# A two-layer decoder trunk on one core: the instruction order made with the scheduler's other machine model

## The chip, the cores and the metric

The kernel runs on one core of one Trainium2 chip. The metric is the device time of one execution in microseconds (us), as the median of several runs. Engines are named as in the profile: PE (TensorE, the matrix engine; its weight loads are PEld), DVE (VectorE), ACT (ScalarE), POOL (GpSimd), SP (SyncE, which here only issues transfers; SPq is its queue).

## The reference, cut to what matters

Two layers of a decoder over 256 tokens of width 1024, all in float32. Each layer runs three token mixers on the same input and adds them through gates, then a feed-forward network:

```
p = x @ w_in[l]                                   # one wide projection for all mixers
y_a = rwkv7_time_mix(...)                         # recurrence over tokens, 8 heads of 64
y_b = mla_branch(...)                             # latent attention, 8 heads, blocks of 128 queries
y_c = s5_branch(...)                              # diagonal state space, 32 groups x 64 states
merged = g0 * y_a + g1 * y_b + g2 * y_c           # sigmoid gates, also from p
x = layer_norm(ALPHA * x + merged @ w_out[l])
h = silu(x @ ffn_w1[l]) * (x @ ffn_w3[l])         # width 2816
x = layer_norm(ALPHA * x + h @ ffn_w2[l])
```

## The kernel before, in words

**The weight stream.** Almost all of the matrix work is one stream of weight chunks of 128 x 1024 floats (512 KB), 138 a layer, in the order in which the program uses them. `w_load` (lines 156 to 173) handles one chunk: SyncE issues its load into `raw` (line 160, three buffers), ScalarE casts it to a rounded high part `whi` (line 161), and VectorE subtracts to get the low part `wlo` (line 171; for some chunks GpSimd takes the last eighths, line 173). `whi` and `wlo` have four buffers each. A projection (`mm3`, lines 206 to 208) makes three matmuls for each 128 x 128 block: high times high, high times the input's low part, low times high. One chunk in this form is 8 blocks, 24 matmuls of 256 columns.

**The stages of a layer.** First the inputs of the mixers are projected (`rw_unit`, `s5_in`, `latents`), with the state space scan (`s5_tile`, lines 717 to 774) between. Then comes the mixing stage, a list of steps in `ORDER2`: preparation of the recurrence (`prep`), its scores, the inverse of its triangular blocks (`inverse`), its `solve` (lines 1018 to 1077), its normalization (`norm`, line 1103 near its end), attention, and projections and gates of the stream (`glu_unit`, `branch1`, `gate_pair`, `branch0`). `branch0`, four chunks a layer, needs the recurrence's result; the other projections don't. Then `token_major` multiplies by `w_out` (lines 510 to 512) and applies the layer norm, the feed-forward network's first part runs in 22 pieces, and `token_major` again multiplies by `ffn_w2`.

**A solve** goes over four blocks of 64 tokens, one after the other. In each, TensorE makes a right-hand side (lines 1031 and 1035), ScalarE copies it from PSUM into `Gc`, TensorE multiplies it by the inverse (line 1043), VectorE copies the result into `ST`, and for three of the four blocks TensorE makes the next state (lines 1053 and 1055), which VectorE scales in two halves (line 1059). There are two solves in each layer.

**The tables of the state space model.** `s5_tables` builds them; for layer 1 GpSimd does it during layer 0's feed-forward stage (lines 384 to 389 are the rotation that doubles the cosine and sine tables). For layer 0 the work is shared, with VectorE and ScalarE taking part (lines 404 to 418).

**What sets the order.** The program is written in one order, and every instruction gets its rank from its place there. When the `TileContext` closes, a scheduler puts the instructions of each engine into their final order. It plays the program through on a model of the machine: whenever the model says that an engine can take an instruction, the scheduler gives it, among those whose inputs and buffers the model says are there, the one that comes first in the program. The order so found is fixed in the program; on the chip each engine takes its instructions strictly in that order and waits at the head for what is not there yet. SyncE's transfers are ordered in the same way, so a load that waits for its buffer holds up the loads behind it. In `token_major`, lines 516 to 518 load the two rows of the layer norm and the tokens; their buffers in the feed-forward stage of layer 0 lie where the tables' temporary tiles lay.

A few instructions tie the order by hand: `gate` (in `w_load` and `layer_norm`) makes some chunk subtractions wait for a layer norm's statistics, and `issue_after` keeps four ScalarE instructions behind another.

## Time and profile before

| | |
|---|---|
| time, median of 3 runs | 1072.03 us (1067.92 to 1077.68) |
| the profiled execution's own time | 1068.97 us |
| its span, first to last instruction | 1067.1 us |
| granted TensorE clock, mean | 0.986 of full |
| PE, PEld, DVE, ACT, POOL busy | 1014.2, 912.5, 784.7, 482.6, 235.2 us |
| read from memory | 156.72 MB, 151 GB/s over the span |

The times are device times; the span is what the trace covers, 1.9 us less than that execution's time. Busy time is time in which at least one instruction of the engine is in flight. Matmuls overlap in a pipeline, so a busy TensorE is not one at its peak.

### The profile page before, as it was taken

The numbers are of one execution on the slowest core, as the hardware profiler recorded it, in microseconds if no ns is written. First come the engines' busy times: TensorE is split into PE (matmuls) and PEld (weight loads), VectorE is DVE, ScalarE is ACT, GpSimd is POOL, SyncE is SP. The second block draws the span as 40 slices with busy tenths as digits, with TensorE's granted clock in tenths as the row PEclk, the third lists the DMA queues.
The fourth block names the chain that finished last, engine by engine and source line by source line (L and its number), as shares of the span: only waits on it lengthen the run. The fifth ranks groups of instructions, "written<-read, shape, count | busy, mean of one in ns | idle before, by whom it ended". The sixth has DMA issues, their size and how long they took to land.

```text
span 1067.1 us, 21219 instructions
## 1 busy us (share of the span) xinstructions
PE 1014.2 (95%) x8560; PEld 912.5 (86%) x8560; DVE 784.7 (74%) x1542; ACT 482.6 (45%) x797; POOL 235.2 (22%) x262
## 2 busy tenths in 40 slices
PE   8799989999999999799999999999999999999997
PEld 7798778888896999798878999778889879999885
DVE  7969978976578778386474998888747876667546
ACT  5544477534244244144325346865334423443431
POOL 2970222300000599500012003221002420000000
PEclk9989999999999999999999999999999999999999
DMA  8442241223385555466536325232234755555562
GB/s 280 156 159 90 91 147 41 92 89 100 93 294 177 197 180 171 162 207 217 185 123 218 126 81 191 79 98 85 76 100 173 252 190 215 183 188 183 179 196 79
DMA packets 47394, 163.86 MB, mean 154 GB/s; under 512 B 5696, under 2 KB 8256, under 8 KB 46400
## 3 DMA queue, kind: packets, MB, share of 16 engines
q1 hardware_dynamic: 47008, 161.98, 45.9%
q8 instruction: 67, 1.10, 0.4%
q10 hardware_dynamic: 288, 0.52, 0.1%
q14 instruction: 31, 0.25, 0.1%
HBM read 156.72 MB, written 4.19 MB: 151 GB/s over the span
## 4 chain that ended last, share of the span: by engine, by line
PE 58%; DVE 17%; POOL 9%; DMA 7%; ACT 5%; issue 3%; SPq 0%; DVEq 0%; ACTq 0%; POOLq 0%
PE mm L208 11%; PE mm L207 10%; PE mm L206 10%; DMA raw<-in_ws 6%; DVE wlo L171 3%; PE mm L511 3%; PE mm L512 3%; PE mm L510 3%; ACT whi L161 3%; DVE z L745 1%; PE pa L726 1%; PE pb L1035 1%; POOL st L387 1%; PE pb L1043 1%; PE pa L940 1%
## 5 line engine op out<-in xcount | busy, mean ns | idle before, releaser
L171 DVE TENSOR_TENSOR wlo<-raw,whi 128x1024 fp32r<-128x1024 f32 (+2 forms) x265 | 333.5, 1262 | 171.8 <-ACT whi L161 169.1
L161 ACT CAST whi<-raw 128x1024 fp32r<-128x1024 f32 (+2 forms) x267 | 277.4, 1043 | 379.8 <-PE mm L207 211.8
L206 PE MATMUL mm<-xh,whi 128*128 128x256 f32 x1312 | 376.9, 287 | 14.2 <-ACT whi L161 13.9
L208 PE MATMUL mm<-xh,wlo 128*128 128x256 f32 x1312 | 376.1, 287 | 2.9 <-DVE wlo L171 2.6
L207 PE MATMUL mm<-xl,whi 128*128 128x256 f32 x1312 | 375.1, 286 | 0.4 <-DVE xl L262 0.4
L206 PEld LDWEIGHTS mm<-xh,whi 128*128 128x128 f32 x1312 | 249.2, 190 | 18.6 <-ACT whi L161 14.5
L208 PEld LDWEIGHTS mm<-xh,wlo 128*128 128x128 f32 x1312 | 250.2, 191 | 7.6 <-DVE wlo L171 4.0
L207 PEld LDWEIGHTS mm<-xl,whi 128*128 128x128 f32 x1312 | 250.2, 191 | 2.7 <-DVE xl L262 0.6
L240 POOL TENSOR_TENSOR rs<-rs,mhalf 128x1 f32<-128x1 f32 x8 | 7.8, 971 | 341.2 <-DVE rs L238 341.2
L206 PE MATMUL mm<-yh,whi 128*128 128x256 f32 x256 | 74.6, 291 | 0.1
L207 PE MATMUL mm<-yl,whi 128*128 128x256 f32 x256 | 74.1, 289 | 0.0
L208 PE MATMUL mm<-yh,wlo 128*128 128x256 f32 x256 | 74.1, 289 | 0.0
L511 PE MATMUL mm<-wlo,hh 128*128 128x512 f32 x132 | 52.0, 394 | 0.0
L510 PE MATMUL mm<-whi,hh 128*128 128x512 f32 x132 | 51.7, 394 | 0.0
L512 PE MATMUL mm<-whi,hl 128*128 128x512 f32 x132 | 51.5, 392 | 0.0
L206 PEld LDWEIGHTS mm<-yh,whi 128*128 128x128 f32 x256 | 48.5, 189 | 2.3 <-ACT qa L113 0.9
L207 PEld LDWEIGHTS mm<-yl,whi 128*128 128x128 f32 x256 | 48.5, 190 | 1.2 <-issue 0.8
L208 PEld LDWEIGHTS mm<-yh,wlo 128*128 128x128 f32 x256 | 48.6, 190 | 1.1 <-issue 0.7
L240 POOL TENSOR_TENSOR rsn<-rsn,mhalf 128x8 f32<-128x8 f32 x4 | 6.5, 1634 | 142.8 <-DVE rsn L238 142.8
L173 POOL TENSOR_TENSOR wlo<-raw,whi 128x384 fp32r<-128x384 f32 (+2 forms) x24 | 27.7, 1162 | 44.6 <-ACT whi L161 42.5
L947 POOL TENSOR_SCALAR_AFFINE_SELECT Mk<-Mk 64x512 f32<-64x512 f32 x32 | 27.0, 844 | 43.6 <-ACT Mk L113 42.3
L510 PEld LDWEIGHTS mm<-whi,hh 128*128 128x128 f32 x132 | 24.8, 188 | 6.2 <-DVE th L1284 0.8
(487 smaller groups left out, 1745.7 us busy)
## 6 DMA issues: line engine op xcount, KB each, us to landing
raw<-in_ws SPq DMA_DIRECT2D x267, 512.0 KB, 3.8
raw<-in_ws SPq DMA_DIRECT2D x8, 416.0 KB, 3.5
xd<-xk SPq DMA_DIRECT2D x3, 1024.0 KB, 4.1
xk<-xd SPq DMA_DIRECT2D x3, 1024.0 KB, 7.4
lg<-in_lnv SPq DMA_DIRECT2D x4, 512.0 KB, 5.0
lb<-in_lnv SPq DMA_DIRECT2D x4, 512.0 KB, 5.7
pc<-in_spC SPq DMA_DIRECT2D x2, 768.0 KB, 5.3
pb<-in_spB SPq DMA_DIRECT2D x2, 512.0 KB, 4.9
```

What stands on the lines that cost most here:

```text
L161: S.copy(out=hi[:, s], in_=raw[:, s])
L171: V.tensor_tensor(out=lo[:, 0:m], in0=raw[:, 0:m], in1=hi[:, 0:m].bitcast(F32), op=ALU.subtract)
L173: G.tensor_tensor(out=lo[:, m:w], in0=raw[:, m:w], in1=hi[:, m:w].bitcast(F32), op=ALU.subtract)
L206: PE.matmul(ps, lhsT=wh, rhs=xh, start=first, stop=False)
L207: PE.matmul(ps, lhsT=wh, rhs=xl, start=False, stop=False)
L208: PE.matmul(ps, lhsT=wl, rhs=xh, start=False, stop=last)
L240: G.tensor_tensor(out=out, in0=in_, in1=mh(out), op=ALU.pow)
L387: E.tensor_tensor(out=s1, in0=c0, in1=ls, op=ALU.mult)
L510: PE.matmul(acc[b][n], lhsT=ah, rhs=w[0][:, s], start=(k == 0), stop=False)
L511: PE.matmul(acc[b][n], lhsT=ah, rhs=w[1][:, s], start=False, stop=False)
L512: PE.matmul(acc[b][n], lhsT=al, rhs=w[0][:, s], start=False, stop=(k == nk - 1))
L947: G.affine_select(out=Mk[r, h], in_=Mk[r, h], pattern=[[0, 4], [1, 2], [1, 64]], compare_op=ALU.is_ge, fill=0.0, base=-1, channel_multipli ...
```

## The change: one argument of the context

The scheduler has two models of the machine. By default it plays the program on the first, a simulator that runs each instruction for a modelled duration. The argument chooses the second, a timeline simulator with its own durations for instructions, transfers and queues. The program that is traced is the same, instruction by instruction; buffers are given out and waits are set along the new order. Nothing else differs.

```
@@ -1499,7 +1499,7 @@
         arrays[f"in_{name}"] = a
         args.append(nc.dram_tensor(f"in_{name}", a.shape, mybir.dt.from_np(a.dtype), kind="ExternalInput").ap())
     out = nc.dram_tensor("out_0", (T, D), F32, kind="ExternalOutput").ap()
-    with tile.TileContext(nc) as tc:
+    with tile.TileContext(nc, schedule_with_timeline_sim=True) as tc:
         trunk(tc, *args, out)
     r = _run(nc, [arrays], core_ids=[0])
     return r.results[0]["out_0"].reshape(1, T, D)
```

## Rows read from the trace of the kernel before

**Rows 1.** The page's first part: busy us (share of the span) and instructions, each engine.

```profile
span 1067.1 us, 21219 instructions
...
PE 1014.2 (95%) x8560; PEld 912.5 (86%) x8560; DVE 784.7 (74%) x1542; ACT 482.6 (45%) x797; POOL 235.2 (22%) x262
```

**Rows 2.** Windows of 27 us: length, busy time and instructions, clock, DMA.

```profile
108.00:135.00 27.00, 23.21 (x277) 20.28 (x276) 27.00 (x52) 13.19 (x22) 7.30 (x6) 1.00 0.30 96
270.00:297.00 27.00, 25.57 (x243) 23.30 (x242) 14.59 (x24) 8.66 (x13) 1.64 (x1) 1.00 0.40 135
918.00:945.00 27.00, 27.00 (x228) 27.00 (x227) 18.18 (x29) 11.62 (x15) 0.00 (x0) 1.00 0.57 179
```

**Rows 3.** Waits of PE: waiter, awaited, us in total, times, longest.

```profile
PE mm L206 <- ACT whi L161: 13.9, 3, 6.8
PE pc L1094 <- DVE yT L1089: 3.1, 2, 1.7
```

**Rows 4.** Around 442 us: SPq's wait, timelines (start, length) of SP, ACT, PE.

```profile
SPq L516 <- POOL st L389: 15.5, 1, 15.5
...
442.81 0.33 SPq L516 DMA_DIRECT2D lg<-in_lnv  x1
...
452.44 1.04 ACT L161 CAST whi<-raw 128x1024 fp32r<-128x1024 f32 x1 [16.28 <-DMA raw<-in_ws]
...
453.54 0.58 PE L206 MATMUL mm<-xh,whi 128*128 128x256 f32 x1 [6.83 <-ACT whi L161]
```

**Rows 5.** Around 50 us: timelines of ACT and PE.

```profile
48.67 1.33 ACT L418 ACTIVATE cd<-pb,c 128x512 f32<-128x512 f32 x2 [4.98 <-DVE pb L408]
...
51.35 0.58 PE L206 MATMUL mm<-xh,whi 128*128 128x256 f32 x1 [5.62 <-ACT whi L161]
```

**Rows 6.** Windows around the two long waits; the clock follows POOL's busy time.

```profile
42.00:81.00 39.00, 30.94 (x276) 29.41 (x276) 26.35 (x31) 18.54 (x30) 30.63 (x22) 0.82 0.43 147
439.00:467.00 28.00, 20.70 (x157) 20.20 (x156) 11.51 (x19) 7.99 (x10) 3.62 (x3) 0.88 0.63 225
```

**Rows 7.** One solve's block, 271 to 275 us: timeline of all engines.

```profile
271.76 0.44 PE L1035 MATMUL pb<-ST,Mk 64*64 64x64 f32 x4
...
272.30 0.37 ACT L113 COPY Gc<-pb 64x256 f32<-64x256 f32 x1 [5.91 <-PE pb L1035]
...
272.60 0.28 PE L207 MATMUL mm<-xl,whi 128*128 128x256 f32 x1
...
272.80 0.68 PE L1043 MATMUL pb<-Gc,DTf 64*64 64x64 f32 x8
...
273.51 0.43 DVE L113 COPY ST<-pb 64x256 f32<-64x256 f32 x1 [3.18 <-PE pb L1043]
...
274.13 0.28 PE L208 MATMUL mm<-xh,wlo 128*128 128x256 f32 x1
...
274.34 0.27 PE L1055 MATMUL pb<-ST,BKt 128*64 128x64 f32 x1
```

**Rows 8.** Groups by line: count, busy us, mean ns, idle before, its cause.

```profile
L113 DVE COPY ST<-pb 64x256 f32<-64x256 f32 x16 | 6.7, 421 | 24.1 <-PE pb L1043 24.1
...
L1059 DVE TENSOR_TENSOR S<-pb,gam 64x128 f32<-64x128 f32 x24 | 6.9, 289 | 6.5 <-PE pb L1055 6.3
...
L113 ACT COPY Gc<-pb 64x256 f32<-64x256 f32 x16 | 5.9, 366 | 35.2 <-PE pb L1035 35.1
```

**Rows 9.** The weight stream in the feed-forward stage: timeline of PE.

```profile
479.82 0.28 PE L206 MATMUL mm<-xh,whi 128*128 128x256 f32 x1
479.94 0.28 PE L207 MATMUL mm<-xl,whi 128*128 128x256 f32 x1
```

**Rows 10.** The recurrence's last step and the next stage's first (min/median/max ns, first to last start).

```profile
289.65 1.06 PE L1103 MATMUL pc<-dg,pc 128*128 128x256 f32 x4
...
L510 PE MATMUL mm<-whi,msh x24: 388/396/501, 319.3 to 341.2; 128*128 128x512 f32 x24
...
813.24 1.02 PE L1103 MATMUL pc<-dg,pc 128*128 128x256 f32 x4
...
L510 PE MATMUL mm<-whi,msh x24: 387/389/796, 842.7 to 865.6; 128*128 128x512 f32 x24
```

**Rows 11.** Line 171 at 351 to 437 us and at 891 to 1000 us.

```profile
L171 DVE TENSOR_TENSOR wlo<-raw,whi x28: 1210/1378/2287, 350.4 to 433.3; 128x1024 fp32r<-128x1024 f32 x28
...
L171 DVE TENSOR_TENSOR wlo<-raw,whi x38: 1224/1228/1230, 890.6 to 997.1; 128x1024 fp32r<-128x1024 f32 x38
```

More of the change, by code (lines that the diff above doesn't have):

```diff
@@ L1501 @@
     out = nc.dram_tensor("out_0", (T, D), F32, kind="ExternalOutput").ap()
-    with tile.TileContext(nc) as tc:
+    with tile.TileContext(nc, schedule_with_timeline_sim=True) as tc:
         trunk(tc, *args, out)
```

## The prediction

> **What bounds the kernel now.** I read the views from the whole to the single wait. The page's first part: TensorE (PE) has work in flight for 1014.2 of 1067.1 us, 95%, and no other engine comes near [rows 1]. So a new order can hardly win by emptying another engine; it wins or loses in what TensorE does between its first and last matmul. The table of windows then says where those 53 us lie. In the feed-forward stage (918 to 945 us) TensorE is busy 27.00 of 27.00 us at full clock: nothing there is waiting for an order. In the mixing stage (108 to 135, 270 to 297) it is busy 23.21 and 25.57, and in the first of these VectorE (DVE) is full, 27.00 of 27 [rows 2]. The list of waits names one large group: three waits of TensorE for ScalarE's cast of a weight chunk, 13.9 us together, the longest 6.8 [rows 3]. Everything else is under 3.2 us.
>
> Two of these waits are faults of order, and a scheduler's faults are what this change can touch. At 453.54 us TensorE stands 6.83 us. The SyncE queue shows why: its load of the layer-norm row (line 516) waits 15.5 us for GpSimd's table work (line 389), because the row's buffer takes that work's space, and weight loads stand behind it in the same queue; they go out from 444.18 on, and the cast that TensorE needs starts only at 452.44 [rows 4]. The old model believed GpSimd done earlier than it was. At 51.35 us TensorE stands 5.62 us: ScalarE had stood 4.98 us at line 418 for a VectorE result, and the cast was queued behind it [rows 5]. After both, the granted clock is low: 0.82 over 42 to 81 us and 0.88 over 439 to 467, a mean of time at 2.4 and at 1.2 GHz [rows 6].
>
> **What the change does, part by part.** It removes no instruction and adds none: every duration in the trace stays, up to contention. It moves all of them that are free to move, on five engines and on the SyncE queue, which carries all weight loads. What moves is the choice, each time an engine is free, among instructions that the model believes ready. The trace shows one execution of one order, so each term is a price for an order that fits less or better.
>
> *The recurrence's steps.* Here the present order fits closely, and this is the term that decides. Look at the solve at 271 to 275 us: TensorE's step of line 1035 begins its last group at 271.76 and runs 0.44; ScalarE copies its result (0.37); line 1043 starts at 272.80. Between them lie stream matmuls of lines 206 to 208 that fill just this gap, the last starting at 272.60. The same holds across VectorE's copy of 0.43 at 273.51: stream matmuls to 274.13, then line 1055 at 274.34 [rows 7]. The old model puts each step within some 0.2 us of where the chip can take it. There are 16 such copies by ScalarE, 16 by VectorE, and 24 state updates in 12 pairs [rows 8]: 16 + 16 + 12 = 44 round trips from TensorE to another engine and back, 22 a layer.
>
> An order from other durations can miss in two ways. Too early: the step stands at the head while the copy runs, and TensorE idles for the gap that is now filled, 272.20 to 272.80 = 0.6 us; 44 x 0.6 = 26 us, paid in full since TensorE is the bound. Too late: the step stands behind stream matmuls that were ready first. A weight chunk is 24 matmuls (8 blocks, three products) starting 0.12 us apart [rows 9], 2.88 us, so half a chunk is 1.44 us; 22 x 1.44 = 31.7 us a layer on the chain. TensorE does stream work meanwhile, so this costs only what the stream can't cover at the end. That cover is to be seen: the last step of the recurrence (line 1103) is at 289.65 and 813.24, its matmuls through at about 290.7 and 814.3; the next stage (line 510) starts at 319.3 and 842.7 [rows 10]. Of these 28.5 us, 4 chunks (the `branch0` units) need the recurrence's result, 4 x 2.88 = 11.5; the rest, 17 us, can be done earlier. So 31.7 - 17 = 14.6 us a layer, 29 in both. The bounds: 0 if every step is met as well as now, 2 x (22 x 2.88 - 17) = 93 us if each stands behind a whole chunk. I take 29, close to the 26 of the other way of missing. A gain in this stage is not excluded: the page's PE row leaves 53 us in all, and 41 us of it are not the two faults.
>
> *The two faults.* At best both go: 6.83 + 5.62 = 12.5 us, and the half clock after them. The clock is worth at most (1 - 0.82) x 39 = 7 us and (1 - 0.88) x 28 = 3.4 us [rows 6], together 23 us. At worst both stay, 0, or the misplaced load lands elsewhere on a chunk that is needed at once. I take the first gone and the second kept: -6.8.
>
> A page bears on whether the first goes. In this trace VectorE's subtraction of a weight chunk takes a median 1378 ns, up to 2287, while GpSimd builds the tables, and 1228 (1224 to 1230) where GpSimd is idle [rows 11]; so the two engines stretch each other here. The Trainium skill, "SBUF — State Buffer", section "Who interferes with whom", says that a VectorE instruction with two SBUF inputs and a GpSimd instruction that reads SBUF exclude each other, the later one blocking fully. By that rule a model that prices each engine alone, however well, still sees GpSimd finish too early, the load keeps its place, and the sum would be 6.8 us higher.
>
> *The SyncE queue and VectorE.* Loads that change places cost nothing in the feed-forward stage, where chunks lie ready ahead of TensorE [rows 2]. In the mixing stage VectorE is the cover that is gone: at 27.00 of 27 any chunk subtraction that it takes late is late for TensorE by its own 1.2 us [rows 11]. I put 0 for it in the sum and a rival below.
>
> **The sum.** Against the profiled execution's 1068.97 us: -6.8 + 29.2 = 1091.4. The median of the runs shown, 1072.03, is 3.1 above that execution; so 1094.
>
> **Rivals.** *Faster: the other model is nearer to the chip.* Its place is the SyncE queue at 442 us and ScalarE at 48 us; it decides if lines 516 to 518 are issued behind the weight loads and the cast ahead of line 418, while the 44 steps fit as now. Price: -12.5 us alone gives 1060, with the clock 1049. For it: both faults come from wrong durations. Against it: in the recurrence the old durations were right, so there is little to win besides. Chance 0.30.
>
> *No difference.* The new order is nearly the old one, or a fault removed is paid for by a few steps missed (10 steps too early are 6 us): 1061 to 1083, most likely 1069. For it: the feed-forward stage is full whatever the order [rows 2]. Chance 0.28.
>
> *Slower by another way: starved stream.* A load whose buffer is not yet free is put ahead of weight loads, as at 442 us, at two or three more places, at 7 us each: 1086 to 1093. Its mark would be new waits of TensorE for line 161 or 171 over 5 us, with the recurrence unchanged. Chance 0.08.
>
> **How the numbers follow.** The forecast (steps of the recurrence missed) has 0.34, its own range 1083 to 1128: from half its price to nearly twice. The whole range reaches down over no difference and over most of the faster case, to 1046, and up to 1128; outside stay the best of the faster case and whole-chunk misses, 0.2 together. About 1% is what a measurement here can tell from no change (1061 to 1083). Faster by over 1%: 0.30; within 1%: 0.28; slower: 0.34 + 0.08 = 0.42.
>
> **What would show it.** Right: TensorE's busy time per 27 us falls in 190 to 300 and 710 to 820 us; the waits of ScalarE's `Gc` and VectorE's `ST` copies for lines 1035 and 1043, 35.1 and 24.1 us now [rows 8], grow by some tens of us, or TensorE shows new waits for them; line 510 starts over 10 us later than at 319.3 and 842.7. First fault gone: line 516 issued without a 15 us wait, no 6.8 us gap. Wrong: the recurrence's stretch keeps its length, or shrinks, and the time falls with the two gaps.

## The result, and the profile after

The changed kernel takes 1180.05 us in the median (1177.56 to 1182.24), the kernel before, run beside it, 1073.64; the ratio is 1.0977 (95% interval 1.0931 to 1.1023). No instruction was added to or taken from an engine (the counts below are those of before), so these 106 us are all order. The forecast had the sign right and the size wrong: 1094, with 1128 as its upper end.

The page's first part of the kernel after:

```profile
span 1179.3 us, 21250 instructions
...
PE 1057.5 (90%) x8560; PEld 948.8 (80%) x8560; DVE 792.1 (67%) x1542; ACT 482.4 (41%) x797; POOL 231.8 (20%) x262
```

Against [rows 1] TensorE stands still for 121.8 us where it was 52.9, 69 us more, and the same 8560 matmuls are in flight for 43 us longer; together these are the 112 us of the span. TensorE's share falls only from 95% to 90%, so the share hides a good part of the loss. The Trainium skill, "Perfetto Trace Analysis", section "Identifying the Most-Contended Engine", says that TensorE's matmul busy share is not a good measure of how close a kernel is to roofline, because matmuls are pipelined. For comparing two runs the trace adds a second reason, the clock, below.

Where the loss is, is read from stages. The table is worked out from the first and last starts of TensorE's lines in the two traces: line 851 opens the recurrence's preparation, line 1103 closes its normalization, line 490 is the layer norm's transpose, line 1300 the feed-forward network's first transpose, a few microseconds behind its first matmuls. Differences are taken before rounding.

| stage, us | before | after | difference |
|---|---|---|---|
| start to line 851 | 139.5 | 144.2 | +4.7 |
| mixing, layer 0: to the last of 1103 | 150.8 | 213.4 | **+62.5** |
| to the first of 490 (rest of the stream, `w_out`) | 54.4 | 43.4 | -11.0 |
| layer norm, to 1300 | 11.9 | 16.1 | +4.2 |
| feed-forward, to 490 | 193.1 | 194.4 | +1.3 |
| to line 851 of layer 1 | 114.3 | 115.8 | +1.5 |
| mixing, layer 1 | 149.8 | 199.7 | **+49.8** |
| to 490 | 55.1 | 46.6 | -8.5 |
| layer norm | 12.0 | 20.1 | +8.1 |
| feed-forward, to the end | 186.1 | 185.6 | -0.5 |

So the mixing stages lose 112.3 us and the stages right behind them give 19.5 back: stream that had been done early need not be done late. Net, 93 of the 112 us of span; another 12.3 lie in the two layer norms.

Windows of the kernel after: the first and the last answer to the first and the last of [rows 2], between them the bad stretch of layer 0 (217 to 289) and of layer 1 (797 to 865).

```profile
108.00:135.00 27.00, 20.41 (x298) 16.67 (x296) 23.06 (x51) 9.88 (x20) 0.05 (x1) 0.87 0.29 96
217.00:244.00 27.00, 14.61 (x89) 9.96 (x89) 22.62 (x98) 10.26 (x28) 3.15 (x6) 0.55 0.08 29
244.00:271.00 27.00, 18.74 (x242) 14.34 (x242) 14.02 (x59) 8.97 (x28) 2.70 (x4) 0.50 0.00 1
271.00:289.00 18.00, 15.51 (x226) 11.90 (x228) 9.43 (x33) 3.48 (x8) 1.64 (x1) 0.71 0.01 2
797.00:824.00 27.00, 21.19 (x242) 15.41 (x242) 23.37 (x98) 13.44 (x40) 5.85 (x9) 0.75 0.07 21
824.00:865.00 41.00, 31.60 (x371) 24.84 (x372) 21.69 (x88) 8.59 (x24) 1.84 (x2) 0.63 0.01 1
1020.00:1047.00 27.00, 27.00 (x227) 27.00 (x227) 17.86 (x29) 11.67 (x15) 0.00 (x0) 1.00 0.55 182
```

The same windows of layer 0 in the kernel before:

```profile
217.00:244.00 27.00, 26.94 (x256) 21.79 (x257) 17.98 (x74) 9.44 (x21) 1.57 (x1) 1.00 0.31 99
244.00:271.00 27.00, 26.92 (x391) 23.49 (x390) 18.17 (x38) 11.29 (x21) 0.07 (x1) 1.00 0.30 99
271.00:289.00 18.00, 16.57 (x172) 14.69 (x172) 8.44 (x15) 5.24 (x8) 1.64 (x1) 1.00 0.19 61
```

Read the last column, GB/s, first: 1 to 2 GB/s for the last 45 of these 72 us, 29 ahead of them, where before had 61 to 99. The granted clock is 0.50 to 0.71 (0.50 is 1.2 GHz throughout) where it was 1.00 (2.4 GHz), and TensorE is busy 14.61 of 27 us where it was 26.94. The feed-forward window is as full as ever.

The waits of the kernel after (waiter, awaited, us, times, longest):

```profile
PE pa L490 <- DVE xk L483: 11.4, 2, 7.4
PE mm L206 <- ACT whi L161: 8.6, 2, 7.7
PE pa L916 <- DVE BK L908: 8.6, 3, 5.9
PE pb L1043 <- ACT Gc L113: 7.1, 8, 2.0
PE pa L916 <- DVE DT L970: 6.2, 1, 6.2
...
SPq L160 <- DVE wlo L171: 699.6, 190, 78.0
...
SPq L516 <- POOL st L389: 15.3, 1, 15.3
```

And line 171 in 217 to 290 us, by lines:

```profile
L171 DVE TENSOR_TENSOR wlo<-raw,whi x1: 1221/1221/1221, 218.6 to 218.6; 128x1024 fp32r<-128x1024 f32 x1
```

The SyncE queue stands 78.0 us at one weight load (none is issued between 219.86 and 298.22), and between 217 and 290 us VectorE makes a single chunk subtraction, where in the same stretch the kernel before makes 12. The buffers are full and TensorE takes nothing from them.

Why it takes nothing is read from TensorE's sequence. I counted, in the traces, the stream matmuls (lines 206 to 208) that stand between the steps of the preparations, scores and first halves of attention of layer 0, from the first line 916 on (a slash where steps follow each other):

```
before: 916 -5- 926 -1- 1188 -2- 1188/940/1188 -5- 1188 ... 916 -5- 926 -1- 940 -2- 940/1188 -2- 1188/867 -4- 871/891 -61- 916
after:  916 -23- 926 -3- 1188 -23- 1188 -4- 940 -15- 940 -5- 1188 -23- 1188 ... 916 -34- 926 -3- 940 -22- 940/1188 -22- 1188/867 -18- 871/891 -0- 916
```

The old order spends 1 to 5 stream matmuls at the short steps, whose inputs lie ready, and keeps 61 for the long wait, in which VectorE prepares the next operands (891 to 916); 50 more cover the next such wait. The new one puts nearly a whole chunk, mostly 22 or 23 of 24, in front of short steps and has nothing left for these two long waits. There TensorE stands bare (timeline):

```profile
217.66 0.44 PE L891 MATMUL pa<-c,kr 128*128 128x128 f32 x2
224.34 0.88 PE L916 MATMUL pa<-c,BK 128*128 128x128 f32 x3 [6.24 <-DVE DT L970]
...
231.85 0.69 PE L891 MATMUL pa<-c,kr 128*128 128x128 f32 x2
238.41 0.87 PE L916 MATMUL pa<-c,BK 128*128 128x128 f32 x3 [5.87 <-DVE BK L908]
```

"Nothing left" has a reason in the program. From the recurrence's first step on, 387 stream matmuls run until 216.83; what comes next in the stream's order needs attention's result, whose last part line 1221 makes at 288.29. In the old order the stream that is free of that need lasts until 245.3 and attention is done at 244.34. The stream has one fixed order, so what stands behind that piece waits too.

The first solve of each layer then runs alone, with 0 stream matmuls among its steps where before had 64 and 73. Its last block in layer 0 answers to [rows 7]:

```profile
276.48 0.69 PE L1035 MATMUL pb<-ST,Mk 64*64 64x64 f32 x4
...
277.26 0.37 ACT L113 COPY Gc<-pb 64x256 f32<-64x256 f32 x1 [6.46 <-PE pb L1035]
...
277.68 1.11 PE L1043 MATMUL pb<-Gc,DTf 64*64 64x64 f32 x8 [0.51 <-ACT Gc L113]
...
278.83 0.41 DVE L113 COPY ST<-pb 64x256 f32<-64x256 f32 x1 [0.63 <-PE pb L1043]
```

No stream matmul lies in the gaps, and the same groups take 0.69 and 1.11 us instead of 0.44 and 0.68, at the half clock.

The second solve of each layer is the opposite. The piece that needed attention's result is free by then, and the stream that was held up stands between the solve's steps, about a chunk at each (layer 0, stream matmuls between the steps, as above):

```
before: 1035 -11- 1043 -6- 1055 -7- 1031/1035 -5- 1043 -11- 1053/1055 -7- 1031/1035 -4- 1043 -4- 1053/1055 -14- 1031/1035 -4- 1043
after:  1035 -18- 1043 -24- 1055 -25- 1031/1035 -23- 1043 -23- 1053/1055 -24- 1031/1035 -34- 1043 -33- 1053/1055 -24- 1031/1035 -23- 1043
```

From its first line 1035 to its last line 1070 this solve takes 46.9 us where it took 22.2, and 42.8 where it took 21.2 in layer 1. But TensorE loses nothing in it; a window of the kernel after:

```profile
298.70:346.00 47.30, 47.30 (x439) 43.43 (x436) 21.92 (x30) 17.52 (x27) 0.00 (x0) 1.00 0.42 134
```

What it does here need not be done behind the last line 1103: the time from there to line 510 is 14.7 and 13.1 us, where it was 29.0 and 28.8. So the loss is not in these late steps. Most of it lies ahead of them: from line 851 to the end of the first solve the two layers take 137.7 and 126.5 us where they took 97.9 and 97.1, 69 us more, for some 25 stream matmuls more in each.

The groups of line 113 that answer to [rows 8]:

```profile
L113 DVE COPY ST<-pb 64x256 f32<-64x256 f32 x16 | 6.7, 422 | 25.5 <-PE pb L1043 25.3
...
L113 ACT COPY Gc<-pb 64x256 f32<-64x256 f32 x16 | 5.8, 366 | 46.0 <-PE pb L1035 46.0
```

And by lines, with first and last start, those that answer to [rows 10]; the last of line 1103 is at 927.0 where it was at 813.9:

```profile
L1103 PE MATMUL pc<-dg,pc x16: 378/559/766, 299.3 to 927.0; 128*128 128x256 f32 x16
...
L510 PE MATMUL mm<-whi,msh x48: 389/395/629, 372.3 to 963.8; 128*128 128x512 f32 x48
```

The fault of [rows 4] is still there, at 501 us; that of [rows 5] has changed its releaser and lost half a microsecond (timelines):

```profile
52.89 0.58 PE L208 MATMUL mm<-xh,wlo 128*128 128x256 f32 x1 [5.08 <-DVE wlo L171]
...
501.18 0.33 SPq L516 DMA_DIRECT2D lg<-in_lnv  x1
...
511.87 0.58 PE L206 MATMUL mm<-xh,whi 128*128 128x256 f32 x1 [7.69 <-ACT whi L161]
```

### The profile page after: what moved, and what is told of

Read it like the earlier page. It is cut to its first block, busy times and chain, and to the rows that moved or that the text cites. A ratio compares the mean times of both kernels' runs of the same rounds, so it can differ in the third digit from the quotient of the medians.

```text
span 1179.3 us, 21250 instructions
## 1 busy us (share of the span) xinstructions
PE 1057.5 (90%) x8560; PEld 948.8 (80%) x8560; DVE 792.1 (67%) x1542; ACT 482.4 (41%) x797; POOL 231.8 (20%) x262
## 4 chain that ended last, share of the span: by engine, by line
PE 65%; DVE 14%; POOL 8%; ACT 5%; DMA 5%; issue 3%; SPq 0%; DVEq 0%; ACTq 0%; POOLq 0%
PE mm L206 12%; PE mm L207 12%; PE mm L208 12%; DMA raw<-in_ws 4%; PE mm L510 3%; PE mm L511 3%; PE mm L512 3%; DVE wlo L171 2%; ACT whi L161 1%; PE pa L726 1%; PE pb L1043 1%; PE pa L1188 1%; PE pb L1035 1%; PE pb L1031 1%; PE pc L510 1%
## 5 line engine op out<-in xcount | busy, mean ns | idle before, releaser
L206 PEld LDWEIGHTS mm<-xh,whi 128*128 128x128 f32 x1312 | 251.2, 191 | 15.7 <-ACT whi L161 9.0
L173 POOL TENSOR_TENSOR wlo<-raw,whi 128x384 fp32r<-128x384 f32 (+2 forms) x24 | 32.0, 1340 | 94.5 <-ACT whi L161 88.2
L510 PE MATMUL mm<-whi,hh 128*128 128x512 f32 x132 | 47.6, 393 | 0.0
L947 POOL TENSOR_SCALAR_AFFINE_SELECT Mk<-Mk 64x512 f32<-64x512 f32 x32 | 21.9, 684 | 58.4 <-ACT Mk L113 57.1
L512 PEld LDWEIGHTS mm<-whi,hl 128*128 128x128 f32 x132 | 24.8, 188 | 5.5
```

The lines of the kernel that those rows point to most:

```text
L173: G.tensor_tensor(out=lo[:, m:w], in0=raw[:, m:w], in1=hi[:, m:w].bitcast(F32), op=ALU.subtract)
L206: PE.matmul(ps, lhsT=wh, rhs=xh, start=first, stop=False)
L510: PE.matmul(acc[b][n], lhsT=ah, rhs=w[0][:, s], start=(k == 0), stop=False)
L512: PE.matmul(acc[b][n], lhsT=al, rhs=w[0][:, s], start=False, stop=(k == nk - 1))
L947: G.affine_select(out=Mk[r, h], in_=Mk[r, h], pattern=[[0, 4], [1, 2], [1, 64]], compare_op=ALU.is_ge, fill=0.0, base=-1, channel_multipli ...
```

## The experiments

Each kernel is built in two passes. The first reads the order that one model gives each engine; the second gives that order, edited or not, to chosen engines and lets a model order the rest around it. The order is given by dependencies without a semaphore, which bind the scheduler alone; what they cost on the chip is at most what run 1 shows:

```
+ TAKEN, MODEL, ENGINES = False, True, ["PE"]   # whose order (False: old), who orders the rest, which engines
+ for e in ENGINES:
+     names = seq[e]                            # as the model TAKEN has ordered them
+     for a, b in zip(names, names[1:]):
+         tc.add_manual_dep(by[b], a, <NoSync>, reason="order taken")
```

**1. All five orders of before, under the new model.** `TAKEN, MODEL, ENGINES = False, True, all five`.

> The other model stays on, but the order of the kernel before is imposed on all five engines. Theory 1 (the cost lies in the order of TensorE's instructions, which puts steps of the mixing stage behind whole pieces of the weight stream and spends the stream early) and theory 2 (the cost lies in the orders of the other engines) both expect the time of the kernel before, 1065 to 1080 us. If buffers or waits that the other model sets otherwise cost by themselves, without any change of order, the time stays over 1090.

Measured 1075.91, ratio 1.0046 (1.0000 to 1.0092). The change acts through the order; anything else is worth under 1%.

**2. TensorE's old order, the others by the new model.** `ENGINES = ["PE"]`.

> Only TensorE has the order of the kernel before; the four other engines are ordered by the other model around it. Theory 1: most of the 107 us come back, 1070 to 1115, and the stream no longer ends at 217 us in layer 0. Theory 2: little comes back, 1150 to 1185.

Measured 1136.91, ratio 1.0612 (1.0530 to 1.0694): between both expectations. Theory 1 as I had it falls; the other engines' orders, as this model makes them around TensorE's old one, cost some 63 us. Not all of that is a part of after's loss: in the profiled execution, 75 us over that of before, 23.7 us lie ahead of layer 0's line 851, where after loses 4.7.

**3. The four others' old orders, TensorE by the new model.** `ENGINES = ["DVE", "Activation", "SP", "Pool"]`.

> VectorE, ScalarE, GpSimd and SyncE have the order of the kernel before, and TensorE is ordered by the other model around it. Theory 1: most of the cost stays, 1140 to 1185, with a long stretch at the half clock before the last step of the recurrence. Theory 2: 1075 to 1100.

Measured 1178.99, ratio 1.1019 (1.0955 to 1.1084): nothing comes back. TensorE's order is a third one here (3941 of its 8560 places hold the instruction that after has there, and the order of before has 4059): the mixing stages take 194 us each, less than in after, and the stretches behind them give nothing back (57.7 and 53.9 us).

**4. TensorE's new order, the others by the old model.** `TAKEN, MODEL, ENGINES = True, False, ["PE"]`.

> The converse: the old model orders everything, but TensorE has the order of the kernel after. Theory 1: near the kernel after, 1140 to 1185. Theory 2: near the kernel before, 1070 to 1100.

Measured 1188.03, ratio 1.1106 (1.1042 to 1.1170), 3 us over the range of theory 1. TensorE's order alone makes the whole loss (114 us), the others' alone more than half (63), and both together 106. The prices don't add. That both use up the same cover is my reading; no run tried it.

**5. All five old orders, within the mixing stages only.**

```
- for every instruction
+ only where lines.index(851) <= place < lines.index(510) of its layer   # places in the traced program
```

> The other model orders everything, but within the two mixing stages the instructions of all five engines keep the order of the kernel before. Theory 1, that the cost lies in the mixing stages: by the starts of line 851 and of the first layer-norm transposes (line 490) in the two traces the mixing stages with what follows up to there make up 51.6 and 41.3 of the 107 us, so 80 to 100 us come back and the time is 1080 to 1100. Theory 2, that the loss is spread over the whole program and only shows in the mixing stages: 1130 or more.

Measured 1100.70, ratio 1.0217 (1.0168 to 1.0265): 79 us come back, 0.7 us off the expected range. The other 25 (against the first run's 1075.91) lie mostly outside: by the same starts of lines as in the table, 5.3 ahead of layer 0's mixing, 13.0 in the two stretches from line 1103 to 490 and 9.2 in the two layer norms.

**6 and 7. Which of the other engines.** `ENGINES = ["PE", "DVE"]` and `["PE", "Activation", "SP", "Pool"]`.

> TensorE and VectorE have the order of the kernel before; ScalarE, GpSimd and SyncE are ordered by the other model around them. With TensorE alone it was 1137, so the orders of the other four engines cost 63 us by themselves. If VectorE's order is what costs there (chunk subtractions ahead of the steps' own operations, as the waits for lines 908, 749 and 171 suggest): 1070 to 1100. If it is SyncE's or ScalarE's: 1115 to 1140.

> The counterpart: TensorE, ScalarE, GpSimd and SyncE have the order of the kernel before, VectorE alone is ordered by the other model. If VectorE's order is what costs: 1115 to 1140. If it is SyncE's or ScalarE's: 1070 to 1100.

Measured 1102.68, ratio 1.0227 (1.0172 to 1.0283), and 1121.05, ratio 1.0400 (1.0353 to 1.0447). The second is as expected if VectorE's order costs, the first misses that range by 3 us. VectorE's new order alone costs 45 us against the first run, the three others' alone 27; VectorE's is the larger part, and not the only one. But as in run 2 much of it lies where after hardly loses: of the 53 us that the profiled execution of run 7 takes over that of before, 15.1 are ahead of layer 0's mixing stage and 12.1 ahead of layer 1's (run 1, with no order changed, has 7.9 there), against 21.1 in the two mixing stages. Its mark in run 2 is the wait of line 916 for line 908, 13.8 us in five waits: among others the preparation's own operations stand behind chunk subtractions.

**8. Is it the clock?** The orders of after, with 324 matmuls of `ones` by `ones` to columns that nothing reads:

```
+ filler = lambda ps, o, n: [PE.matmul(ps[:, o:o + 128], lhsT=ones, rhs=ones, ...) for _ in range(n)]
+ filler(ps, 256, 3)   # in solve, behind each group; 8 in inverse, 4 (at 384) in attention
```

> The orders of the kernel after on all five engines, plus 324 matmuls without use: 3 behind each group of the solves, 8 behind each group of the inverses and 4 behind each group of transposes in attention, written to columns of the same PSUM tile that nothing reads. Theory 3, that the half clock in the bare stretch is itself a large part of the loss: in 216 to 286 us TensorE is busy 46.9 us at a mean granted clock of 0.56, which at full clock would be about 20 us less, 40 in both layers; the granted clock in these stretches rises to over 0.9 and the time falls to 1140 to 1160. If the waits between the steps decide and the clock is only their sign: 1175 to 1200.

Measured 1261.50, ratio to before 1.1714 (1.1650 to 1.1778), 81 us over the kernel after: both theories miss, and the test is spoilt. A window:

```profile
276.00:290.00 14.00, 12.43 (x66) 9.63 (x64) 5.05 (x28) 0.46 (x2) 0.00 (x0) 0.50 0.01 2
```

The fill by lines, with who waited for it (us, times):

```profile
L143 PE MATMUL pb<-ones x648: 273/275/583, 184.4 to 993.5; 128*128 128x128 f32 x162
...
  ACT Gc L113: 76.5, 14
  DVE ST L113: 55.0, 16
```

The copy out of PSUM waits for the last write to its tile, the fill's, and three fills take 1.65 us (at 276.90) against a copy of 0.37. So the fill lay on the chain, not beside it. What it does show: most of what is added to the bare chain is paid (in the two first solves the fill is in flight for 17.1 and 15.2 us, and they take 14.8 and 9.3 longer), and the clock stayed at 0.50 with TensorE in flight for 12.43 of 14 us.

**9. The forecast's own term.** The kernel before, with TensorE's order edited; the old model orders the rest.

```
+ for each group of LATE = (1031, 1035, 1043, 1053, 1055) in the mixing stages:
+     emit BACK = 12 stream matmuls first, drawn forward in their order,
+     stopping at a piece that needs the recurrence's or attention's unfinished result
```

> The kernel before with one edit of TensorE's order: in the mixing stages each group of the two solves (lines 1031 to 1055) stands behind 12 matmuls of the stream, half a chunk, counted from the group ahead of it, as long as stream that doesn't need the recurrence's result is left; the old model orders the other engines around it. This is the term of the forecast by itself. By the forecast's working 29 us in both layers, 1095 to 1110. If the stream left for the end covers it: 1070 to 1082. If bare steps at the end cost more than the working has, through the half clock and loads that stop: over 1115.

Measured 1097.14, ratio 1.0242 (1.0190 to 1.0295): 24 us, as expected. The total agrees with the working, its parts do not. The working has 31.7 us a layer on the chain, of which 17 come back at the end. The mixing stages grow by 14.6 and 10.7 us only, since the steps had stream ahead of them already (64 to 73 matmuls in a solve of before, 73 to 120 here), and nothing comes back: from the last line 1103 to line 510 it is 29.8 and 29.3 us, where it was 29.0 and 28.8. In place of that TensorE stands behind the second solve, where the stream that covered VectorE's work is now spent:

```profile
299.51 1.11 PE L1094 MATMUL pc<-c,yT 128*128 128x128 f32 x4 [5.80 <-DVE yT L1089]
```

So the agreement is in part luck.

**10. The same lateness ahead of the solve.** `LATE = (916, 926, 940, 1188)`, `BACK = 12`. The words put on record name line 921; the kernel that ran has line 1188, the first half of attention, in its place.

> The same edit, half a chunk of stream ahead of each group, put instead to the end of each preparation (lines 916, 921, 926) and to the scores (line 940), which come before the inverse and the solve; about as many stream matmuls are drawn forward (453 against 438). Theory 1 as the trace of after has it (lateness ahead of the solve costs more, because the inverse and the solve behind it then stand bare): over 1110 and over the run with the late solve. If only the sum of the delays counts, whichever step has them: within 10 us of that run.

Measured 1130.05, ratio 1.0579 (1.0507 to 1.0652): 57 us for about as many matmuls drawn forward. Windows of runs 9 and 10, in this order:

```profile
217.00:244.00 27.00, 25.04 (x237) 21.01 (x236) 17.31 (x73) 6.30 (x14) 0.00 (x0) 0.87 0.30 95
```

```profile
217.00:244.00 27.00, 19.90 (x275) 17.04 (x276) 10.88 (x32) 11.73 (x34) 2.69 (x4) 0.64 0.06 21
```

Late preparations, scores and attention leave the stretch of after, half clock and stopped loads included; late solve steps hardly do.

**11 and 12. A better order of before?** All five old orders, with small edits.

```
  SP:         lines 516, 517, 518 (layer 0, second token_major) moved behind the next 12 of line 160
  and in 12,  ACT: last two of line 418 behind the next three casts;
              DVE: 406, 409, 408 each behind one of the next three chunk subtractions
```

> The kernel before with the three loads of lines 516 to 518 (layer 0, second token_major) put behind the next twelve weight loads on SyncE; nothing else moves. If the wait at 442 us costs what the forecast had: 6.8 us less, up to 3.4 more with the clock, 1063 to 1068. If SyncE's queue or VectorE stops TensorE at another place instead: 1070 to 1076.

> The same, and at 48 us ScalarE's last two of line 418 behind the next three casts, with VectorE's table lines 406, 409 and 408 between the subtractions of the next chunks. If both stalls go: 10 to 20 us less than the kernel before, 1054 to 1064. If VectorE, which is full there, is what TensorE waits for in the end: no less than the run with the first stall mended alone.

Measured 1070.08, ratio 0.9969 (0.9936 to 1.0002), and 1071.09, ratio 0.9981 (0.9946 to 1.0016): no difference that holds, against the first expectation of each. Windows of run 11 (the first answers to the second of [rows 6]), then the second of them in before:

```profile
439.00:467.00 28.00, 28.00 (x236) 28.00 (x235) 20.63 (x31) 11.86 (x15) 2.63 (x2) 1.00 0.62 207
...
570.00:600.00 30.00, 27.00 (x168) 25.09 (x166) 15.67 (x27) 11.11 (x18) 0.00 (x0) 0.77 0.44 143
```

```profile
570.00:600.00 30.00, 27.74 (x224) 26.49 (x222) 18.98 (x30) 15.47 (x26) 1.37 (x1) 1.00 0.55 177
```

The stall is gone, 28.00 of 28.00. Part comes back in the second `token_major` (476.3 to 541.5 us, 65.2, where before took 61.3), which leaves 5.3 us for the feed-forward stage (187.8 where it was 193.1). In this execution the clock then falls at 575 us, after a wait that before has too, and the stretch to line 851 takes 121.8 where it was 114.3. So the time of the whole can't tell what the fault itself was worth. In run 12 the early stall goes and line 442 waits 6.94 us at 66.05 for a ScalarE copy instead.

**13. Whole chunks at the short steps.** As run 9, `LATE = (926, 940, 1188)`, `BACK = 24`.

> The kernel before with one edit of TensorE's order, as the trace of after has it: in the mixing stages each group of lines 926, 940 and 1188 (end of a preparation, scores, first half of attention) stands behind 24 matmuls of the stream, a whole chunk, where before it was 1 to 6; the old model orders the other engines around it. If whole chunks at these short steps are what the new order does to the kernel: 1145 to 1190, with the stream gone by about 215 us in layer 0 as in after. If lateness at these steps is worth no more than the half chunk was: 1120 to 1140.

Measured 1143.27, ratio 1.0640 (1.0571 to 1.0709): 67 us, 2 us below the range. The stretch of after, in run 13, by windows and on the timeline:

```profile
200.00:217.00 17.00, 7.63 (x36) 4.83 (x34) 14.52 (x71) 8.02 (x26) 3.22 (x6) 0.73 0.14 50
217.00:244.00 27.00, 18.66 (x260) 14.90 (x260) 15.79 (x53) 10.27 (x29) 5.34 (x8) 0.63 0.00 1
```

```profile
213.71 0.87 PE L916 MATMUL pa<-c,BK 128*128 128x128 f32 x3 [7.84 <-DVE DT L970]
```

One edit of TensorE's order makes after's picture: the bare wait at line 916, 1 GB/s, the half clock. It is smaller, and so is what is drawn forward: in run 13, 288 stream matmuls are spent by 199 us and 64 are left among the steps of layer 0's first solve, where after has spent all 387 and has none there. Its second solves are those of before (22.2 and 21.2 us); whole chunks at their steps, which after has, were not tried by themselves.

**14. The reverse.** The kernel after, `ENGINES = ["PE"]` with the old order, in the mixing stages only (as in run 5).

> The kernel after, but TensorE's instructions of the two mixing stages keep the order of the kernel before; TensorE elsewhere and all of the other engines are ordered by the other model. With TensorE's old order everywhere the mixing stages were 165.5 and 168 us long (line 851 to the last of line 1103) against 213.4 and 199.7 in after; with what the next stages give back that is about 60 us less than after. If TensorE's order in the mixing stages is the main cause: 1105 to 1135. If the orders of the other engines undo the repair: over 1150.

Measured 1137.17, ratio 1.0583 (1.0506 to 1.0660): 43 us come back, as much as with TensorE's old order everywhere (run 2), and 2 us short of the expected. So its old order outside the mixing stages brings nothing more, though the two runs are not alike by stages: ahead of layer 0's mixing stage run 2 takes 163.2 us and run 14 145.1. With run 5, another 36 us need the other engines' old orders in the mixing stages as well.

## Why the prediction missed

**The bound** was read rightly: no other engine became it, the feed-forward stage stayed full, and what changed is what TensorE does between its first and last matmul.

**The failed step** is the one that I called the term that decides, the recurrence's steps. It priced the 22 round trips of the solves, each behind half a chunk, 14.6 us a layer (its parts give 14.7), and put every step ahead of the solves at nothing: preparation, scores, attention. I counted the solves because rows 7 and 8 show them; for leaving out the rest the working gives no reason. The loss is where the term has nothing: 69 us up to the end of the first solves. There the new order puts whole chunks (22 to 24 matmuls) ahead of steps whose inputs lie ready. Half a chunk there costs 57 us (run 10) and a whole one at fewer steps 67 (run 13), where half a chunk at the solve's steps costs 24 (run 9). It not only delays the chain: it spends the cover of the long VectorE waits on steps that needed none, until the stream comes to a piece that needs the delayed chain itself. Then inverse and first solve run with nothing beside them.

Of the solves' own steps, half had no stream in front of them, those of the first solve, and half a whole chunk, those of the second. There the forecast's mechanism took place, at twice its size, and cost TensorE almost nothing: 47.30 of 47.30 us in flight. The cover at the end, put at 17 us a layer, was read rightly, with 14.3 and 15.7 us given back; after it the longest wait at line 1094 is 4.2 us, where before has 1.7. So the lateness that I priced was covered, and the lateness that I left out was not.

The upper bound of that term, 93 us for whole chunks at all steps of the solves, is also what the two mixing stages cost net. That is chance, since the loss lies at other steps. But whole chunks should have been a case with its own chance, as a chunk is the unit in which the program writes the stream; I had left it outside the range because nothing in the trace of before showed how late a step would be.

**The two faults.** I took the first as gone, at -6.8; it stayed, 7.69 us. The Trainium skill's rule from "SBUF — State Buffer", "Who interferes with whom", had pointed that way, and the trace agrees in the outcome, GpSimd's table work still being awaited for 15.3 us; that the exclusion of the two engines is the cause was not tried. The second I took as kept, and it was, with another releaser. Run 11 adds that the first fault gone gave 3.3 us in the whole, in an interval that reaches to none, and 5.3 in its own stage, not 6.8.

**VectorE at nothing** was wrong: its new order costs 45 us without the others'; how much of the loss in after it makes, beside TensorE's, that does not tell. The mark was in rows 2, 27.00 of 27.00 us, and I gave it neither a price nor a rival of its own. I also read that window, 108 to 135 us, as the mixing stage; it lies ahead of it (line 851 starts at 139.5), in the projections and the scan.

**The marks.** TensorE's busy time fell in the two stretches named, line 510 starts 53.0 us later in layer 0, and `Gc` waits 10.8 us longer; that is less than the tens of us named, and `ST`, named with it, waits only 1.4 longer. The rival of a starved stream had the time of 7 us a place; the stream was starved, but by TensorE's own order through full buffers.

**What stays open** is how much of the loss is the half clock. Over the whole span the granted clock is 0.919 where it was 0.986, and the same matmuls are in flight for 43 us longer; the other 69 us are time in which TensorE stands. If TensorE's busy time in 217 to 289 us had been at full clock it would be (1 - 0.55) x 14.61 + 0.50 x 18.74 + (1 - 0.71) x 15.51 = 20.4 us less, an upper estimate for layer 0, where the net loss is 51.6. Run 8, meant to settle it, could not.

## What to carry to other kernels

Where independent work fills the gaps of a chain, that work is a stock, and an order is good if it spends the stock on the long waits; count, between consecutive steps of the chain, how much filler stands there and whether the step's input was ready. A step that is late costs little itself, as the second solves show, as long as the filler in front of it had to be done anyway and other filler is not missed later; what it takes from a later, longer wait is the price, and if the filler further on needs the chain's result, both stop together. Prices of two bad orders need not add (114 and 63 us made 106 here), so undoing one part tells only what is left with the other part in place. And a total that agrees with a forecast is not yet a mechanism that agrees: compare by stages, as in run 9.

## Not expected of the hardware

After TensorE stood 2.26 us at 581.61 in the kernel before, the granted clock over 570 to 600 us was 1.00; after 3.00 us at the same place in run 11 it was 0.77, and after 3.09 us in run 1, with the same orders as before, 0.72. In run 1 the clock was still at a mean of 0.59 in this window, in which TensorE was in flight all the time:

```profile
585.00:600.00 15.00, 15.00 (x75) 13.88 (x75) 7.06 (x12) 3.68 (x5) 0.00 (x0) 0.59 0.31 115
```

From the first of line 623 to line 851 of layer 1 the kernel before took 113.0 us and run 1 121.0. A fall of the clock at one wait can so make some 8 us of the spread of the kernel before, 1062.83 to 1082.39 us beside runs 11 and 12; that it does in the other executions was not looked at.
